# Delta rule of a hybrid layer: the preparations of two pairs of heads made together instead of one after the other

## The chip, the core and the metric

The kernel runs on one core of one Trainium2 chip. The core has a matmul engine (PE, with its weight loads shown apart as PEld), VectorE (DVE), ScalarE (ACT), GpSimd (POOL), and queues that issue DMA transfers (SPq, ACTq). All data are float32. The metric is the device time of one execution in microseconds (us), lower is better.

## The reference

The layer has two token mixers behind one normalisation and one input projection: a gated delta rule of 4 heads, and a dilated attention of 8 heads. Their outputs, each gated, go through one output projection and are added to the input. The sequence has 2048 tokens and 1024 channels. The change touches the delta rule alone. For each head it works on 32 chunks of 64 tokens:

```python
gc = jnp.cumsum(g.reshape(b, h, n, CHUNK), axis=-1)
diff = gc[..., :, None] - gc[..., None, :]
decay = jnp.exp(jnp.where(tril_incl, diff, -jnp.inf))
kb = kc * bc[..., None]
a_mat = jnp.where(tril_strict, jnp.einsum('bhnid,bhnjd->bhnij', kb, kc) * decay, 0.0)
l_mat = a_mat + jnp.eye(CHUNK, dtype=a_mat.dtype)
u = lax.linalg.triangular_solve(l_mat, vc * bc[..., None], ...)
w = lax.linalg.triangular_solve(l_mat, kb * jnp.exp(gc)[..., None], ...)
attn_intra = jnp.einsum('bhnid,bhnjd->bhnij', qc, kc) * decay
...
def step(state, inp):
    v_new = u_i - w_i @ state
    o_i = qd_i @ state + a_i @ v_new
    state = state * gl_i + kt_i.T @ v_new
```

Here `l_mat` is a 64x64 triangular matrix per chunk and head. The chunks of a head follow each other through `state`.

## The kernel before

The 4 heads are two pairs. The two heads of a pair lie side by side on the 128 partitions (64 each, `s_` counts them), and 4 chunks (`u`) are prepared at a time, so there are 8 groups of 4 chunks for each pair. The work has these stages.

1. **The input projection** (`conv_proj`, lines 460 to 481, and `gate_proj`): 128x128x512 products on PE, lines 206 to 208 (tile `pj`), then the short convolution on DVE and ACT.
2. **The products k k** (`stage1a`, lines 501 to 533), run while the projection goes on: for one pair and 4 chunks, k is loaded (`kT1`, one buffer), 8 products of 64 columns each go into one PSUM bank of tile `A` (line 514), and DVE makes the decayed matrix from it. It is called 16 times.
3. **The inverse** (`inverse`, lines 535 to 554): of each 64x64 triangular matrix the two 32x32 diagonal blocks are inverted, on DVE for the first half of the sequence and on POOL for the second, and stored to memory.
4. **The preparation** (`stage2`, lines 614 to 711), for one pair and 4 chunks at a time, 16 times. It loads k, q, v, the decays and the blocks of the inverse into `TTz` (line 643) and `D0t` (line 644). `TTz` exists twice, one for each call in turn, so in effect one for each pair. The missing 32x32 block of the inverse takes two products: 8 products of 32x32 (line 650), a copy by DVE (`Xs`, line 653), 8 more products (line 657), and a copy by ACT with a minus sign into `TTz` (line 660). Then come q k (line 665), the norms of q (line 668, in the bank of the 32x32 products), transposes of k and v (line 688), and the two products with the inverse (lines 701 and 707), the second of which reads `TTz` last. All of these use tile `A` of the pool `psD`, which has two PSUM banks. Its results `WQ`, `Ks`, `U` and `at_` have three buffers each.
5. **The chain** (`chain`, lines 720 to 747): for each chunk and pair, products with the state (line 727), new values (DVE, line 731), the state's update (PE line 733, DVE line 737), and the output (PE line 741, ACT and DVE). The update products of both pairs share one bank, `SU`.
6. **The attention**, whose projection (`proj_fill`, tile `pj`, issued through the helper at line 99) fills PE while the delta rule runs. At most 5 x 192 of its products may be issued before the last product of the chain (`HOLD`, lines 963 and 964). After that the attention's own steps begin, and then the output projection.

The order of the instructions on each engine is fixed when the kernel is compiled: a scheduler takes, among the instructions that it holds to be ready by its own estimate of times, the one of the highest priority (the lowest number in `tc.cur_priority`). Chain and outputs start from 1,000,000, the preparation from 1,200,000, the attention's projection from 2,400,000. From the attention on (`pin[0] = True`, line 839) the order within each engine is as written. `add_manual_dep(..., NOSYNC)` sets the order of two instructions of one engine and adds no wait.

The loop that starts the preparations (lines 783 to 793) runs over the groups: the chain's first chunk of both pairs, then the next group's preparation for pair 0 and for pair 1, then the other three chunks.

Of the kernel before, what the change touches and what calls it, by code (L numbers as in the profile page):

```python
# [8 lines left out]
F32 = mybir.dt.float32  # L9
# [7 lines left out]
P = 128  # L17
# [7 lines left out]
NOSYNC = mybir.DependencyInfo(mybir.DependencyClass.NoSync, mybir.DependencyReason.DATA)  # L25
CH = 64
# [54 lines left out]
def dap(t, off, dims):  # L81
    return bass.AP(tensor=t.tensor, offset=t.offset + off, ap=[list(d) for d in dims])


def hybrid(tc, xT, x, norm_w, w_in, conv_w, a_log, dt_bias, dn_norm_w, q_norm_w, k_norm_w,
# [37 lines left out]
    dma = nc.sync.dma_start  # L123
    adma = nc.scalar.dma_start

    dr, _ = pool("dr", space=DRAM)
    qkvT_d = [[dr.tile([P, 32, 2, CH], F32, name=f"cv{w}{p}") for p in range(2)] for w in range(3)]
# [91 lines left out]
    nc = engines  # L219
    dma = nc.sync.dma_start  # L220
    adma = nc.scalar.dma_start
# [4 lines left out]
    for _ in range(14):  # L226
# [5 lines left out]
                                                        bufs=3 if b + g < 2 else 1) for n in ("wh", "wl"))  # L232
# [94 lines left out]
    for kt in range(KT):  # L327
# [14 lines left out]
        for i in range(4):  # L342
            for j, (x_, w_) in enumerate(((xh, 0), (xh, 1), (xl, 0))):
                nc.tensor.matmul(pz[i][:, :260], x_[0][:, kt, i * P:(i + 1) * P], wz[0][kt][w_][:, kt % 4, :260],
                                 start=kt == 0 and j == 0, stop=kt == KT - 1 and j == 2)
# [4 lines left out]
    for g, (tb, b, i) in enumerate(groups):  # L350
# [12 lines left out]
        k = g if tb == 0 else (g - 4) % 8  # L363
# [21 lines left out]
    nc = tc.nc  # L385
    dma = nc.sync.dma_start
    adma = nc.scalar.dma_start
# [12 lines left out]
    at = ba[:, 4:8, :]  # L400
# [57 lines left out]
    mid, mid_g = pool("mid", side="right")  # L458
# [39 lines left out]

    psD, psD_g = pool("psD", space=PSUM)

    def stage1a(pair, c0):
        hf, cc = divmod(c0, 16)
        u0 = pair * 32 + c0
        kT = mid.tile([P, 4, 2, CH], F32, name="kT1", bufs=1)
        dma(kT, qkvT_d[1][pair][:, c0:c0 + 4])
        gcr = mid.tile([P, 4 * CH], F32, name="t0", bufs=2)
        for s_ in range(2):
            dma(gcr[s_ * CH:(s_ + 1) * CH, :],
                dap(rows_d, (2 * pair + s_) * S + c0 * CH, [[0, CH], [1, 256]]))
        kk = psD.tile([P, 4, CH], F32, name="A", bufs=2)  # L510
        for u in range(4):
            for s_ in range(2):
                ks = kT[:, u, s_]
                nc.tensor.matmul(kk[s_ * CH:(s_ + 1) * CH, u, :], ks, ks, start=True, stop=True)
        pr0 = tc.cur_priority
        tc.cur_priority = pr0 + PE1A
        a4 = mid.tile([P, 4 * CH], F32, name="t1", bufs=2).rearrange("p (u i) -> p u i", u=4)
        E = mid.tile([P, 4 * CH], F32, name="t2", bufs=3).rearrange("p (u i) -> p u i", u=4)
        for u in range(4):
            nc.vector.tensor_tensor_reduce(out=a4[:, u], in0=kk[:, u], in1=id64, scale=1.0, scalar=0.0,  # L520
                                           op0=ALU.mult, op1=ALU.add, accum_out=ssqk[:, u0 + u:u0 + u + 1])
            nc.vector.scalar_tensor_tensor(E[:, u], gcr[:, u * CH:(u + 1) * CH], gc_u[:, u0 + u:u0 + u + 1], mneg,
                                           op0=ALU.subtract, op1=ALU.add)
        nc.scalar.activation(E, E, AF.Exp)
        sA = sA_u[:, u0:u0 + 4]
        nc.vector.tensor_scalar(sA, ssqk[:, u0:u0 + 4], EPS, None, op0=ALU.add)
        nc.vector.reciprocal(sA, sA)
        nc.vector.tensor_tensor(sA, sA, beta_u[:, u0:u0 + 4], op=ALU.mult)
        nc.vector.tensor_tensor(E, E, sA[:, :, None].to_broadcast([P, 4, CH]), op=ALU.mult)
        nc.vector.tensor_tensor(a4, kk, E, op=ALU.mult)  # L530
        dma(A_d[hf][pair, cc:cc + 4].rearrange("u p i -> p u i"), a4)
        dma(Es_d[hf][pair, cc:cc + 4].rearrange("u p i -> p u i"), E)
        tc.cur_priority = pr0
# [23 lines left out]
    for hf in range(2):  # L557
        tc.cur_priority = PR1A[hf]
        for c in range(0, 16, 4):
            for p_ in range(2):  # L560
                stage1a(p_, hf * 16 + c)
        tc.cur_priority = PRINV[hf]
        inverse(hf)

    close(mid_g)
    mid, mid_g = pool("mid2", side="right")
# [14 lines left out]
    dn, dn_g = pool("dn")  # L581
# [29 lines left out]
    turn2 = [0]  # L611
    SU = psD.tile([P, 4, P], F32, name="SU", bufs=1)

    def stage2(pair, c0, dma2=dma):

        hf, cc = divmod(c0, 16)
        u0 = pair * 32 + c0
# [3 lines left out]
        kT = dn.tile([P, 4, 2, CH], F32, name="kT", bufs=2)  # L623
        qT = dn.tile([P, 4, 2, CH], F32, name="qT", bufs=2)
        vT = dn.tile([P, 4, 2, CH], F32, name="vT", bufs=1)
# [4 lines left out]
        for s_ in range(2):  # L630
            d0 = dma(Qr[:, :, s_], dap(rows_d, (12 + 2 * pair + s_) * S + c0 * CH, [[0, P], [CH, 4], [1, CH]]))
        WQ = dn.tile([P, 4, 2, P], F32, name="WQ", bufs=3)
# [3 lines left out]
        E = dn.tile([P, 4, CH], F32, name="E2", bufs=2)  # L636
        dma2(E, Es_d[hf][pair, cc:cc + 4].rearrange("u p i -> p u i"))
        TT = TTz[n2 % 2]
        D0 = dn.tile([P, 4, 32], F32, name="D0t", bufs=2)
        Xs = dn.tile([P, 4, 32], F32, name="Xs", bufs=1)  # L640
        for s_ in range(2):
            a = s_ * CH
            dma2(TT[a:a + CH, :, a:a + CH], A_d[hf][pair, cc:cc + 4, a:a + CH].rearrange("u p i -> p u i"))
            dma2(D0[a:a + 32], dap(D0_d[hf], (m0 + s_) * 1024, [[32, 32], [2048, 4], [1, 32]]))
        pa = psD.tile([P, 512], F32, name="A", bufs=2)
        px, pn = pa[:, :256].rearrange("p (a u i) -> p a u i", a=2, u=4), pa[:, 256:260]
        for u in range(4):
            for s_ in range(2):
                a, b = s_ * CH, s_ * CH + 32
                nc.tensor.matmul(px[b:b + 32, 0, u], TT[a:a + 32, u, b:b + 32], D0[a:a + 32, u], start=True, stop=True)  # L650
        for s_ in range(2):
            b = s_ * CH + 32
            nc.vector.tensor_copy(Xs[b:b + 32], px[b:b + 32, 0])
        for u in range(4):
            for s_ in range(2):
                a, b = s_ * CH, s_ * CH + 32
                nc.tensor.matmul(px[a:a + 32, 1, u], Xs[b:b + 32, u], TT[b:b + 32, u, b:b + 32], start=True, stop=True)
        for s_ in range(2):
            a = s_ * CH
            nc.scalar.mul(TT[a:a + 32, :, a + 32:a + 64], px[a:a + 32, 1], -1.0)  # L660
        q2 = dn.tile([P, 4, P], F32, name="tmp", bufs=2)
        nc.scalar.activation(q2, qT.rearrange("p u s i -> p u (s i)"), AF.Square)
        pq = psD.tile([P, 4, P], F32, name="A", bufs=2)
        for u in range(4):
            nc.tensor.matmul(pq[:, u], kT[:, u].rearrange("p s i -> p (s i)"), qT[:, u].rearrange("p s i -> p (s i)"),  # L665
                             start=True, stop=True)
        for u in range(4):
            nc.tensor.matmul(pn[:, u:u + 1], q2[:, u], one, start=True, stop=True)
        at_ = dn.tile([P, 4, P], F32, name="at_", bufs=3)
        nc.gpsimd.memset(at_[:CH, :, :CH], 0.0)  # L670
        nc.gpsimd.memset(at_[CH:, :, CH:], 0.0)
        for s_ in range(2):
            a, b = slice(s_ * CH, (s_ + 1) * CH), slice((1 - s_) * CH, (2 - s_) * CH)
# [6 lines left out]
        Ks = dn.tile([P, 4, 2, P], F32, name="Ks", bufs=3)  # L680
# [4 lines left out]
        for w, src in enumerate((kT, vT)):  # L685
# [3 lines left out]
            if w == 0:  # L689
                for u in range(4):  # L690
                    nc.scalar.mul(Kc[:, u], tp[:, u], negc_u[:, u0 + u:u0 + u + 1])
                for s_ in range(2):
                    a = slice(s_ * CH, (s_ + 1) * CH)
# [8 lines left out]
        for s_ in range(2):  # L702
            a = slice(s_ * CH, (s_ + 1) * CH)
# [4 lines left out]
        U = dn.tile([P, 4, P], F32, name="U", bufs=3)  # L708
        nc.scalar.copy(U, pu)
        o4 = dn.tile([P, 4, P], F32, name="o4", bufs=2)  # L710
        return dict(WQ=WQ, at=at_, Ks=Ks, U=U, o4=o4, D0=d0)

    Sst = []
    mark = {}
# [57 lines left out]
    def at_prio(k, f, *args):  # L772
        tc.cur_priority = prio[k]
        r = f(*args)
        prio[k] = tc.cur_priority
        return r

    G = {}
    last_D0 = []
    for p_ in range(2):  # L780
        G[p_] = at_prio("prep", stage2, p_, 0, adma)
    last_D0 = [G[1]["D0"]]
    for c0 in range(0, 32, 4):
        cur = dict(G)
        for u in range(4):
            for p_ in range(2):
                at_prio("chain", chain, p_, c0 + u, cur[p_])
            if u == 0:
                for p_ in range(2):
                    if c0 + 4 < 32:  # L790
                        G[p_] = at_prio("prep", stage2, p_, c0 + 4)
        for p_ in range(2):
            z = at_prio("out", dn_out, p_, c0, cur[p_])
        if c0 < 12:
            at_prio("out", bias_out, c0 // 4, z)
# [44 lines left out]
    nc = engines  # L840
    dma = nc.sync.dma_start
    adma = nc.scalar.dma_start
# [393 lines left out]
    G = [heads(hf, p) for hf in range(2) for p in range(4)]  # L1236
# [5 lines left out]
    at, at_g = pool("at")  # L1242
# [23 lines left out]
    for i, g in enumerate(G):  # L1266
        b = 12 * i
# [216 lines left out]
    g = G[7]  # L1484
# [11 lines left out]
    last, part = {}, {}  # L1496
# [56 lines left out]
```

## Time and profile before

| what | value |
|---|---|
| median of 3 runs | 1397.85 us (1396.52 to 1399.55) |
| the profiled execution's own time | 1397.04 us |
| its span, first to last instruction | 1395.2 us |
| DVE busy | 855.7 us (61%) |
| ACT busy | 677.6 us (49%) |
| POOL busy | 486.2 us (35%) |
| k k products on PE (line 514) | 162.2 to 322.9 us of the span |
| delta rule, preparations and chain | 456.5 to 778.5 us of the span |

The profile gives, for one execution, the busy time of each engine, who waited for whom, the chain of work that ended last, and a timeline of instructions. In the timeline an entry starts with its start time and its length in us; "x16" is sixteen records merged into one entry. A float32 product of this stage leaves two records. Products on PE overlap: each lasts longer than the distance to the next one's start, so what a product costs is read from start to start, and not from its length. The projection's products (lines 206 to 208 and `pj` at line 99) work on operands split in two parts and leave one record each.

### The profile page before, as it was taken

The page shows a single profiled execution, that of the slowest core. Times are in us where ns is not written, and L with a number is a line of the kernel's source. Part 1 is how long each engine was busy: PE and PEld are TensorE (multiplying, and loading weights), DVE is VectorE, ACT ScalarE, POOL GpSimd, SP SyncE. Part 2 cuts the span into 40 slices and gives each one's busy share as a digit, 9 for nine tenths or more (in the row PEclk, how much of TensorE's full clock was granted, in tenths as well). Part 3 has the DMA queues.
Part 4 walks back from the last instruction along what each step waited for, and adds up shares of the span by engine and source line. Part 5 has one row for each costly group of instructions (what it writes and reads, how often), then busy time and mean ns, then how long its engine had stood idle before and what let it go on. Part 6 is the DMA issues. An engine that isn't in the chain of part 4 may idle for free.

```text
span 1395.2 us, 28823 instructions
## 1 busy us (share of the span) xinstructions
PE 1362.5 (98%) x10262; PEld 1216.4 (87%) x10262; DVE 855.7 (61%) x2724; ACT 677.6 (49%) x1930; POOL 486.2 (35%) x572
## 2 busy tenths in 40 slices
PE   8999999999999999999999899999999999999998
PEld 7998787778888789999999889999998788888877
DVE  7535667799742358777787564635454746556464
ACT  5644425572321334444444476666556555555520
POOL 3000000000752113442343523575757385654500
PEclk9999999999999999999999999999999999999999
DMA  6654536756547736557553455273647685665764
GB/s 189 184 109 85 109 69 143 159 125 118 102 105 136 201 96 153 158 155 185 138 151 83 103 135 138 69 196 98 161 129 220 177 266 144 211 176 166 204 187 145
DMA packets 301323, 205.01 MB, mean 147 GB/s; under 512 B 149323, under 2 KB 271067, under 8 KB 300668
## 3 DMA queue, kind: packets, MB, share of 16 engines
q1 hardware_dynamic: 231372, 171.11, 49.6%
q10 hardware_dynamic: 69808, 32.06, 8.4%
q8 instruction: 81, 1.33, 0.4%
q14 instruction: 62, 0.51, 0.1%
HBM read 142.61 MB, written 60.50 MB: 146 GB/s over the span
## 4 chain that ended last, share of the span: by engine, by line
PE 80%; DVE 7%; DMA 4%; ACT 3%; POOL 2%; issue 2%; SPq 1%; ACTq 0%; DVEq 0%; POOLq 0%
PE pj L99 16%; PE po L99 10%; PE pj L207 7%; PE pj L208 7%; PE pj L206 7%; PE sc L99 7%; PE pz L99 6%; PE pv L99 4%; PE pt L99 4%; PE SU L733 2%; PE C L727 2%; ACT pr L99 1%; POOL Fb L99 1%; PE A L665 1%; PE pm L99 1%
## 5 line engine op out<-in xcount | busy, mean ns | idle before, releaser
L99 ACT ACTIVATE pr<-pr,ml 128x192 f32<-128x192 f32 (+2 forms) x384 | 156.8, 410 | 160.8 <-DVE ml L99 155.9
L99 PE MATMUL pj<-wh,xh 128*128 128x256 f32 (+1 forms) x776 | 227.1, 293 | 3.6 <-DVE t L99 2.3
L99 PE MATMUL pj<-wh,xl 128*128 128x256 f32 (+1 forms) x776 | 224.6, 289 | 0.0
L99 PE MATMUL pj<-wl,xh 128*128 128x256 f32 (+1 forms) x776 | 224.3, 289 | 0.0
L208 PE MATMUL pj<-xh,wl 128*128 128x512 f32 x512 | 203.5, 397 | 0.7 <-DVE wl L192 0.7
L206 PE MATMUL pj<-xh,wh 128*128 128x512 f32 x512 | 202.6, 396 | 0.0
L207 PE MATMUL pj<-xl,wh 128*128 128x512 f32 x512 | 202.6, 396 | 0.0
L99 PE MATMUL po<-xh,mh 128*128 128x512 f32 x424 | 148.5, 413 | 5.3 <-ACT mh L99 4.2
L99 PEld LDWEIGHTS pj<-wh,xh 128*128 128x128 f32 x776 | 146.4, 189 | 5.0 <-DVE t L99 2.7
L99 DVE CUSTOM_DVE_ANT_0 pr<-sc,bias 128x192 f32<-128x192 f32 (+2 forms) x384 | 100.1, 308 | 77.6 <-PE sc L99 76.7
L99 PEld LDWEIGHTS pj<-wh,xl 128*128 128x128 f32 x776 | 146.5, 189 | 0.5 <-issue 0.3
L99 PEld LDWEIGHTS pj<-wl,xh 128*128 128x128 f32 x776 | 146.6, 189 | 0.1
L478 DVE SCALAR_TENSOR_TENSOR cy<-cu,cw,cy 128x512 f32<-128x512 f32 x144 | 112.1, 778 | 19.8 <-ACT cy L476 17.8
L208 PEld LDWEIGHTS pj<-xh,wl 128*128 128x128 f32 x512 | 96.2, 188 | 23.4 <-DVE wl L192 1.1
L207 PEld LDWEIGHTS pj<-xl,wh 128*128 128x128 f32 x512 | 96.2, 188 | 22.1
L206 PEld LDWEIGHTS pj<-xh,wh 128*128 128x128 f32 x512 | 96.3, 188 | 21.7
L99 POOL COPY qz<-q 64x512 f32<-64x512 f32 x96 | 95.8, 998 | 54.0 <-PE sc L99 43.9
L99 DVE COPY pT<-pt 64x128 f32<-64x128 f32 (+2 forms) x220 | 69.4, 323 | 62.6 <-PE pt L99 59.1
L99 PEld LDWEIGHTS po<-xh,mh 128*128 128x128 f32 x424 | 78.0, 189 | 19.4 <-ACT mh L99 4.8
L99 POOL TENSOR_TENSOR Fb<-Fb,op 128x256 f32<-128x256 f32 x84 | 71.6, 866 | 60.1 <-DMA Fb<-F 59.5
L543 POOL MEMSET inv<- 128x1024 f32 x1 | 1.0, 955 | 260.0 <-ACT wh L191 260.0
L99 PE MATMUL po<-xl,mh 128*128 128x512 f32 x212 | 86.9, 410 | 0.0
(369 smaller groups left out, 3066.3 us busy)
## 6 DMA issues: line engine op xcount, KB each, us to landing
wraw<-in_w_in SPq DMA_DIRECT2D x44, 512.0 KB, 7.2
cv<-cy ACTq DMA_DIRECT2D x48, 256.0 KB, 2.6
Fb<-F SPq DMA_DIRECT2D x64, 192.0 KB, 5.6
xr<-in_xT SPq DMA_DIRECT2D x32, 256.0 KB, 4.0
kT<-cv SPq DMA_DIRECT2D x32, 256.0 KB, 3.5
qk<-qs ACTq DMA_DIRECT2D x64, 128.0 KB, 4.0
res<-in_x SPq DMA_DIRECT2D x13, 512.0 KB, 5.5
V<-v_d SPq DMA_DIRECT2D x20, 256.0 KB, 4.1
```

Of the source, the lines that this page charges most:

```text
L99: i = f(*args, **kw)
L206: nc.tensor.matmul(ps, wh[:, k, c * P:(c + 1) * P], xh[tb][:, kt, :], start=kt == 0, stop=False)
L207: nc.tensor.matmul(ps, wh[:, k, c * P:(c + 1) * P], xl[tb][:, kt, :], start=False, stop=False)
L208: nc.tensor.matmul(ps, wl[:, k, c * P:(c + 1) * P], xh[tb][:, kt, :], start=False, stop=kt == KT - 1)
L478: nc.vector.scalar_tensor_tensor(y, u[:, i:i + 512], cw[:, ct, i:i + 1], y, op0=ALU.mult, op1=ALU.add)
L543: eng.memset(Tt, 0.0)
L665: nc.tensor.matmul(pq[:, u], kT[:, u].rearrange("p s i -> p (s i)"), qT[:, u].rearrange("p s i -> p (s i)"), start=True, stop=True)
L727: nc.tensor.matmul(pc[:, s_], g["WQ"][:, u, s_], S0[:, s_], start=True, stop=True)
L733: nc.tensor.matmul(su[:, s_], g["Ks"][:, u, s_], VN, start=True, stop=True)
```

## The change

Three things are done for both pairs at once that were done for one pair at a time.

- The k k products of both pairs (32 records where there were 16) go into one PSUM bank of tile `A` in a new function `stage1k`; `stage1a` gets its half of the bank. `kT1` has two buffers instead of one.
- `stage2` is split into `stage2_load`, `stage2_blocks` and `stage2_rest`. The loads of both pairs come first, then the 32x32 products of both, then the rest of pair 0 and the rest of pair 1.
- In `stage2_blocks` the 16 first products (line 650 before), those of pair 1 ahead of those of pair 0, and the 16 second products (line 657 before) are each tied in order with `add_manual_dep(..., NOSYNC)`. One copy by DVE for each half of the partitions takes both pairs' blocks. Both pairs' norms of q lie in that same bank, which comes free when both have been read.

```diff
-    def stage1a(pair, c0):
+    def stage1k(c0):
+        kk = psD.tile([P, 2, 4, CH], F32, name="A", bufs=2)
+        for pair in range(2):
+            kT = mid.tile([P, 4, 2, CH], F32, name="kT1", bufs=2)
+            dma(kT, qkvT_d[1][pair][:, c0:c0 + 4])
+            for u in range(4):
+                for s_ in range(2):
+                    ks = kT[:, u, s_]
+                    nc.tensor.matmul(kk[s_ * CH:(s_ + 1) * CH, pair, u, :], ks, ks, start=True, stop=True)
+        return kk
+
+    def stage1a(pair, c0, kk):
-        kT = mid.tile([P, 4, 2, CH], F32, name="kT1", bufs=1)
-        dma(kT, qkvT_d[1][pair][:, c0:c0 + 4])
+        kk = kk[:, pair]
-        kk = psD.tile([P, 4, CH], F32, name="A", bufs=2)
-        for u in range(4):
-            for s_ in range(2):
-                ks = kT[:, u, s_]
-                nc.tensor.matmul(kk[s_ * CH:(s_ + 1) * CH, u, :], ks, ks, start=True, stop=True)
...
-    def stage2(pair, c0, dma2=dma):
+    def stage2(c0, dma2=dma):
+        g = [stage2_load(p_, c0, dma2) for p_ in range(2)]
+        stage2_blocks(g)
+        return [stage2_rest(p_, c0, g[p_]) for p_ in range(2)]
+
+    def stage2_load(pair, c0, dma2):
...
+    def stage2_blocks(g):
         pa = psD.tile([P, 512], F32, name="A", bufs=2)
-        px, pn = pa[:, :256].rearrange("p (a u i) -> p a u i", a=2, u=4), pa[:, 256:260]
+        px = pa[:, :256].rearrange("p (w u i) -> p w u i", w=2, u=4)
+        Xs = dn.tile([P, 2, 4, 32], F32, name="Xs", bufs=1)
+        last = []
+
+        def row(m):
+            if last:
+                tc.add_manual_dep(m.ins, last[-1].ins.name, NOSYNC, reason="in a row")
+            last.append(m)
+
+        for w in (1, 0):
+            TT, D0 = g[w]["TT"], g[w]["D0_"]
+            for u in range(4):
+                for s_ in range(2):
+                    a, b = s_ * CH, s_ * CH + 32
+                    row(nc.tensor.matmul(px[b:b + 32, w, u], TT[a:a + 32, u, b:b + 32], D0[a:a + 32, u], start=True,
+                                         stop=True))
         for s_ in range(2):
             b = s_ * CH + 32
-            nc.vector.tensor_copy(Xs[b:b + 32], px[b:b + 32, 0])
+            nc.vector.tensor_copy(Xs[b:b + 32], px[b:b + 32])
+        for w in range(2):
+            TT = g[w]["TT"]
+            g[w]["pn"] = pa[:, 256 + 4 * w:260 + 4 * w]
+            for u in range(4):
+                for s_ in range(2):
+                    a, b = s_ * CH, s_ * CH + 32
+                    row(nc.tensor.matmul(px[a:a + 32, w, u], Xs[b:b + 32, w, u], TT[b:b + 32, u, b:b + 32], start=True,
+                                         stop=True))
+        for w in range(2):
             for s_ in range(2):
-                a, b = s_ * CH, s_ * CH + 32
-                nc.tensor.matmul(px[a:a + 32, 1, u], Xs[b:b + 32, u], TT[b:b + 32, u, b:b + 32], start=True, stop=True)
...
+                a = s_ * CH
+                nc.scalar.mul(g[w]["TT"][a:a + 32, :, a + 32:a + 64], px[a:a + 32, w], -1.0)
+
+    def stage2_rest(pair, c0, g):
...
-    for p_ in range(2):
-        G[p_] = at_prio("prep", stage2, p_, 0, adma)
+    G[0], G[1] = at_prio("prep", stage2, 0, adma)
...
-                for p_ in range(2):
-                    if c0 + 4 < 32:
-                        G[p_] = at_prio("prep", stage2, p_, c0 + 4)
+                if c0 + 4 < 32:
+                    G[0], G[1] = at_prio("prep", stage2, c0 + 4)
```

More of the change, by code (lines that the diff above doesn't have):

```diff
@@ L559, in hybrid @@
         for c in range(0, 16, 4):
+            kk = stage1k(hf * 16 + c)
             for p_ in range(2):
-                stage1a(p_, hf * 16 + c)
+                stage1a(p_, hf * 16 + c, kk)
         tc.cur_priority = PRINV[hf]
@@ L644, in stage2 @@
             dma2(D0[a:a + 32], dap(D0_d[hf], (m0 + s_) * 1024, [[32, 32], [2048, 4], [1, 32]]))
+        return dict(kT=kT, qT=qT, vT=vT, WQ=WQ, E=E, TT=TT, D0_=D0, D0=d0)
+    def stage2_blocks(g):
         pa = psD.tile([P, 512], F32, name="A", bufs=2)
-        px, pn = pa[:, :256].rearrange("p (a u i) -> p a u i", a=2, u=4), pa[:, 256:260]
-        for u in range(4):
-            for s_ in range(2):
-                a, b = s_ * CH, s_ * CH + 32
-                nc.tensor.matmul(px[b:b + 32, 0, u], TT[a:a + 32, u, b:b + 32], D0[a:a + 32, u], start=True, stop=True)
+        px = pa[:, :256].rearrange("p (w u i) -> p w u i", w=2, u=4)
[12 more added lines that the diff above has]
+                                         stop=True))
@@ L651, in stage2 @@
         for s_ in range(2):
             b = s_ * CH + 32
-            nc.vector.tensor_copy(Xs[b:b + 32], px[b:b + 32, 0])
-        for u in range(4):
-            for s_ in range(2):
[L656 to L660, printed above, removed]
+            nc.vector.tensor_copy(Xs[b:b + 32], px[b:b + 32])
@@ L661, in stage2 @@
+    def stage2_rest(pair, c0, g):
+        hf, cc = divmod(c0, 16)
+        u0 = pair * 32 + c0
+        kT, qT, vT, WQ, E, TT = (g[k] for k in ("kT", "qT", "vT", "WQ", "E", "TT"))
+        pn = g["pn"]
         q2 = dn.tile([P, 4, P], F32, name="tmp", bufs=2)
@@ L710, in stage2 @@
         o4 = dn.tile([P, 4, P], F32, name="o4", bufs=2)
-        return dict(WQ=WQ, at=at_, Ks=Ks, U=U, o4=o4, D0=d0)
+        return dict(WQ=WQ, at=at_, Ks=Ks, U=U, o4=o4, D0=g["D0"])
     Sst = []
```

## The prediction

> **What bounds the kernel now.** I read the page first, for the engine that sets the pace.
>
> ```profile
> span 1395.2 us, 28823 instructions
> PE 1362.5 (98%) x10262; PEld 1216.4 (87%) x10262; DVE 855.7 (61%) x2724; ACT 677.6 (49%) x1930; POOL 486.2 (35%) x572
> ```
>
> PE is busy nearly all the time. Since products overlap, that says only that PE is never long without one. So I asked for the busy times of three stretches (columns: stretch, its length, then busy time and count of PE, PEld, DVE, ACT, POOL, the granted clock, DMA), and for the waits of PE from 150 to 800 us (time in total, times, longest).
>
> ```profile
> 150.00:330.00 180.00, 178.88 (x969) 141.20 (x968) 143.32 (x471) 91.97 (x114) 0.00 (x0) 1.00 0.59 125
> 520.00:766.00 246.00, 246.00 (x2411) 240.63 (x2407) 190.00 (x581) 111.91 (x364) 92.15 (x132) 1.00 0.58 145
> 766.30:778.30 12.00, 8.58 (x58) 6.81 (x56) 10.27 (x32) 3.60 (x14) 2.84 (x3) 1.00 0.49 56
> ```
> ```profile
> PE A L650 <- DMA D0t<-D: 1.8, 1, 1.8
> ```
>
> The first stretch holds the k k products, the second nearly all of the delta rule, the third its end. From 520 to 766 PE waits for nobody, at full clock, with DVE at 190 of 246 us. In these two stages the time is the sum of what PE's instructions cost from start to start: an instruction made cheaper there is time won, and a faster DVE, ACT or POOL is worth nothing. The third stretch is the exception: the attention's products are used up (the mark in the projection forbids more), and the last chunks of the chain run alone. PE issues 58 records there; at 0.11 us each (from the rows below) that is 6.4 of the 12.0 us, so 5.6 us are lost. The longest single wait of the delta rule is 1.8 us, at the first 32x32 product, for a load.
>
> **The edits, one by one.** No product is removed: the same records are regrouped. So what counts is what a group costs beside its records. First the k k products:
>
> ```profile
> 220.23 0.40 PE L207 MATMUL pj<-xl,wh 128*128 128x512 f32 x1
> 220.46 0.39 PE L208 MATMUL pj<-xh,wl 128*128 128x512 f32 x1
> 220.78 0.69 PE L514 MATMUL A<-kT 128*64 128x64 f32 x16
> 221.40 0.50 PE L206 MATMUL pj<-xh,wh 128*128 128x512 f32 x1
> 221.74 0.39 PE L207 MATMUL pj<-xl,wh 128*128 128x512 f32 x1
> ```
> ```profile
> 162.17 0.57 PE L514 MATMUL A<-kT 128*64 128x64 f32 x12
> 162.67 0.50 PE L208 MATMUL pj<-xh,wl 128*128 128x512 f32 x1
> ...
> 322.49 0.69 PE L514 MATMUL A<-kT 128*64 128x64 f32 x16
> ```
>
> Large products follow each other by 0.23 us (220.23 to 220.46). Into the row the step is 0.32, so 0.09 more; the row takes 0.62; the step after the first large product behind it is 0.34, 0.11 more. A row of 12 takes 0.50 (162.17 to 162.67), so four records cost 0.12, 0.03 each; sixteen make 0.48, and 0.14 of the 0.62 is not theirs. A row costs 0.09 + 0.14 + 0.11 = 0.34 us beside its records. The timeline has 17 such rows, the first at 162.17 and the last at 322.49. Joined they are 8, since both pairs' loads lie well ahead of the bank that they wait for: 9 x 0.34 = **3.1 us saved**. The second `kT1` buffer removes a wait that hardly shows. The bank is held longer, but DVE, which empties it, does the same work in the same order.
>
> Now the 32x32 products.
>
> ```profile
> L650 PE MATMUL A<-D0t,TTz 32*32 32x32 f32 x256 | 8.1, 194 | 1.8 <-DMA D0t<-D 1.8
> L657 PE MATMUL A<-TTz,Xs 32*32 32x32 f32 x256 | 7.9, 194 | 0.0
> ```
> ```profile
> 555.52 0.61 PE L727 MATMUL C<-S,WQ 128*128 128x128 f32 x4
> 555.97 0.61 PE L707 MATMUL A<-tmp,TTz 128*128 128x128 f32 x4
> 556.51 0.44 PE L650 MATMUL A<-D0t,TTz 32*32 32x32 f32 x16
> 556.88 0.38 PE L99 MATMUL pj<-wh,xh 128*128 128x256 f32 x1
> 557.10 0.28 PE L99 MATMUL pj<-wl,xh 128*128 128x256 f32 x1
> 557.22 0.28 PE L99 MATMUL pj<-wh,xl 128*128 128x256 f32 x1
> ```
> ```profile
> 456.54 0.21 PE L650 MATMUL A<-D0t,TTz 32*32 32x32 f32 x2 [1.78 <-DMA D0t<-D]
> ...
> 597.02 0.31 PE L657 MATMUL A<-TTz,Xs 32*32 32x32 f32 x6
> ...
> 598.12 0.37 PE L657 MATMUL A<-TTz,Xs 32*32 32x32 f32 x10
> ...
> 744.51 0.24 PE L657 MATMUL A<-TTz,Xs 32*32 32x32 f32 x2
> 744.68 0.94 PE L665 MATMUL A<-qT,kT 128*128 128x128 f32 x6
> ```
>
> There are 16 x 8 products of each kind, two records each. Four records of 128x128 take 0.45 (555.52 to 555.97), 0.11 each; before the row they take 0.54, so 0.09 for going in. The row takes 0.37. Behind it a step is 0.22 where 0.12 is usual: 0.10. A row of two takes 0.17 (744.51 to 744.68), so fourteen records more cost 0.20, 0.0143 each; sixteen make 0.23, and 0.14 of 0.37 is not theirs. One row costs 0.09 + 0.14 + 0.10 = 0.33 us beside its records, more than the records themselves. The Trainium skill, "TensorE: Matmul & The Clock Gate", section "Wait — 56ns, not 53.3ns?", has a floor that would halve this: starts never come closer than about 25 ns, however small the product. By it sixteen records would use up the whole 0.37, a row would cost only 0.19, and the saving below would be 3.6 us; the trace does not agree, with 14 ns per record between the two rows.
>
> The timeline has 41 rows of 32x32 products, the first at 456.54 and the last at 744.51: 32 would do, and 9 of them are cut in two or more, as the one at 597.02 is by products of the chain, which have the higher priority. After the change 16 would do. The tie between neighbours fixes their order but keeps nothing else out, and a row twice as long is cut more often; I take 22. That is 19 x 0.33 = **6.3 us saved** (bounds: 41 rows as now, 0; 16 rows, 8.3).
>
> The `Xs` copies by DVE become half as many and twice as wide, hidden behind PE, as DVE's 190 of 246 us allow.
>
> **What the joining adds.** First, the row now needs the blocks of both pairs. In the first group the second pair's loads are issued on ACT's queue behind the first pair's:
>
> ```profile
> 458.33 0.61 ACTq L644 DMA_DIRECT2D D0t<-D  x1
> ```
>
> By the shortest landing of this line, 1.6 us, that is not there before 459.9, where the row now starts at 456.54. Queued behind it stand all later products; some of the projection can be placed ahead. Between 0 and 4.5 us more waiting: I take **1.5 us lost**, nearest to the 1.78 already there.
>
> ```profile
> L644 ACTq DMA_DIRECT2D D0t<-D x4: 310/613/2042, 447.3 to 458.3; - x4
> ...
> DMA to landing us min/median/max: 1.6/2.8/9.1
> ```
>
> Second, in every later group. `TTz` of pair 1 is read last by line 707, the last product of a preparation. Before, that tile was reloaded while the other pair was prepared, well ahead of its use. Now the joint row of the next group needs it at once. What that takes:
>
> ```profile
> 592.00 0.61 PE L707 MATMUL A<-tmp,TTz 128*128 128x128 f32 x4
> ...
> 592.89 0.44 PE L650 MATMUL A<-D0t,TTz 32*32 32x32 f32 x16
> ```
> ```profile
> 592.64 1.25 SPq L643 DMA_DIRECT2D TTz<-A  x2
> ```
> ```profile
> L643 SPq DMA_DIRECT2D TTz<-A x28: 573/588/1572, 476.9 to 722.8; - x28
> ...
> DMA to landing us min/median/max: 2.3/4.5/9.2
> ```
>
> The next row could so far start 0.45 us behind the last product; now two loads of 0.6 us issue and a landing of 2.3 to 9.2 us lie between. The compile-time order fills that time with the attention's products, but for a landing that it estimates; if the transfer is later, PE stands still with everything behind the row. At nothing if the estimate is generous or the two banks of `A` are busy anyway with the next q k products; at 4.5 - 2.3 = 2.2 us if it counts on the shortest landing and gets the median. Seven groups: 0 to 15 us. I take a third of a microsecond each, **2.5 us lost**, nearer to zero because no other wait of PE stands between 520 and 766.
>
> Third, the end. Of the 5.6 us lost there, some come back if the delta rule's latency falls: four dependent steps fewer in a group (row, copy, row, ACT copy are made once for both). I take **2.5 us saved**, bounds 0 and 5.6; a longer delta rule is the rivals' matter.
>
> **Sum.** -3.1 - 6.3 + 1.5 + 2.5 - 2.5 = -7.9 us. The profiled execution took 1397.04 us (span 1395.2 and 1.8 around it), so 1389.1; the median of the runs lies 0.8 above that execution, which gives **1389.9 us**.
>
> **Rivals.**
>
> *The reload decides (slower).* Each of the seven later rows waits the 2.2 us, nothing is won at the end: -9.4 + 1.5 + 15.4 = +7.5, 1405 us. For it: the first row did wait 1.78 us for just such a load, and landings reach 9.2 us. Against it: an order laid out by the same estimates lets PE wait for no load and no engine between 520 and 766. It decides from 1.1 us a group on, (9.4 - 1.5) / 7. Chance 0.18.
>
> *The rows do not stay whole.* If the chain cuts the longer rows as often per record as now, some 36 remain: 5 x 0.33 + 3.1 = 4.8 saved, less 4.0 of the two waits: 1397 us, no change. For it: 9 cuts now, and a tie that excludes nothing. Against it: most rows of sixteen are whole. Chance 0.16.
>
> *The delta rule gets clearly shorter.* Pair 1's preparation hangs now on the third buffer of `at_`:
>
> ```profile
> L674 DVE TENSOR_TENSOR at__5609<-A,E x2: 416/422/428, 600.2 to 600.6; 64x256 f32<-64x256 f32 x2
> ```
> ```profile
> 611.68 0.59 ACT L709 COPY U<-A 128x512 f32<-128x512 f32 x1 [0.54 <-PE A L707]
> ```
>
> From 600.2 to 612.3 the remaining steps of that pair take 12.1 us. With the blocks and norms of both pairs done early, several of them leave this path, the chain ends before the attention's products run out, and the whole 5.6 us come back, without stalls: -9.4 - 5.6 + 0.5 for the start = -14.5, 1383 us. Chance 0.12.
>
> **How the numbers follow.** The forecast has 0.54. Two thousandths, 2.8 us, is about what a measurement of this kernel can tell from no change. Faster by more: 0.50 of the forecast, 0.07 of the cut rows, 0.12 of the short delta rule: 0.69. Within: 0.04, 0.09 and 0.02 of the reload: 0.15. Slower: 0.16 of the reload. The range runs from 1382, just below the short delta rule, to 1399.5, which leaves out most of the reload's case and nothing else.
>
> **What would show it.** Right: PE waits for nobody from 520 us to the end of the chain but at the joint rows; about 8 rows of 32 k k records and some 22 rows of 32x32 records; a row of 32 takes about 0.60 us from start to start. The reload would show as waits of the first product on `TTz<-A` seven times. Cut rows show as 32x32 rows of less than 32 records between products of lines 727 to 741. A shorter delta rule shows as the attention's products running on past the last product of the chain. I am wrong if the time outside 150 to 790 us moves by more than 2 us, since nothing there is changed.

## The result, and the profile after

| | before | after |
|---|---|---|
| median | 1398.7 us (1396.52 to 1402.04, 4 runs) | 1440.26 us (1433.72 to 1445.3, 4 runs) |
| ratio, 95% interval | | 1.0292 [1.0245, 1.0339] |
| profiled execution | 1397.04 us, span 1395.2 | 1440.5 us, span 1438.7 |
| mean granted clock | 0.997 | 0.984 |

The change makes the kernel 41.6 us slower. The forecast was 1389.9 us, 8 us faster than before; its range ended at 1399.5. The sign was wrong, and the loss lies far beyond every case that the prediction named; the slowest of them was 1405 us.

The page of after, the first lines:

```profile
span 1438.7 us, 28759 instructions
PE 1377.7 (96%) x10262; PEld 1231.4 (86%) x10262; DVE 850.6 (59%) x2708; ACT 668.8 (46%) x1922; POOL 486.9 (34%) x572
```

PE has the same number of records as before, and is busy for 15.2 us more in a span that is 43.5 us longer. The next view, busy times by stretch, says where. The stretch runs from 440 us to the last product of the chain, which ends at 819.2 us where it was 778.3. Columns as in the prediction: stretch, length, busy time and count of PE, PEld, DVE, ACT, POOL, granted clock, DMA. First before, then after.

```profile
440.00:778.30 338.30, 333.10 (x3011) 314.04 (x3009) 236.15 (x705) 140.83 (x442) 112.10 (x163) 1.00 0.59 144
```
```profile
440.00:819.20 379.20, 345.30 (x2989) 324.09 (x2988) 229.83 (x685) 141.15 (x440) 111.47 (x157) 0.95 0.52 127
```

This stretch became 40.9 us longer and holds nearly the whole loss; behind it the kernel takes 619.5 us where it took 616.9. PE's idle time went from 338.30 - 333.10 = 5.2 us to 33.9: 28.7 us more. Its busy time went up by 12.2 us though the stretch holds 22 records fewer: the clock column has 0.95 where it had 1.00. The waits of PE from 440 to 820 us name the instruction:

```profile
PE A L676 <- DMA TTz<-A: 14.9, 4, 5.0
PE A L676 <- DMA D0t<-D: 4.9, 2, 4.0
PE A L676 <- issue: 4.4, 2, 4.2
PE A L739 <- ACT tmp L736: 3.0, 2, 1.7
```

Line 676 is the first joint row (line 650 before). In all it waits 24.2 us, where the prediction's view had one wait of 1.8. Most of it is for `TTz`, the tile whose reload the prediction had taken at 0.36 us a group. The sign of the reload was to be seven such waits. There are four, and a fifth of 4.2 us (at 555.81) that the view can put down to nothing (`issue`); the rows that begin at 511.17 and 692.47 had no such wait. One of the four, in the timeline of PE and in that of the SP queue:

```profile
638.94 1.06 PE L745 MATMUL A<-tmp,TTz 128*128 128x128 f32 x8
...
643.82 0.28 PE L99 MATMUL pj<-wh,xh 128*128 128x256 f32 x1
649.05 0.28 PE L676 MATMUL A<-D0t,TTz 32*32 32x32 f32 x2 [4.96 <-DMA TTz<-A]
649.27 1.65 PE L703 MATMUL A<-qT,kT 128*128 128x128 f32 x6
```
```profile
641.21 1.26 SPq L792 DMA_DIRECT2D zs<-zs_d  x2
642.57 0.57 SPq L99 DMA_DIRECT2D wraw<-in_w_in  x1
643.24 1.24 SPq L655 DMA_DIRECT2D TTz<-A  x2
```

Pair 1's last product (line 745) has read its tile at 640.0. Three other transfers stand ahead of the reload on the queue, which issues at 643.24 and again some 0.6 later, and the row starts at 649.05. From the last product to the row that is 9 us. Until 644.10 the attention's products fill it; the row's place in the order comes then, and PE stands for 5 us. In the waits of the SP queue from 440 to 830 us the reload stood seven times for line 745, 32.7 us in all.

Such a wait can cost more than its length. The granted clock behind the wait that ends at 737.9 us, in stretches of about 2 us of PE alone:

```profile
735.20:737.90 2.70, 0.21 (x2) 0.93 0.75 220
737.90:740.00 2.10, 2.07 (x35) 0.50 0.08 17
740.00:742.00 2.00, 2.00 (x11) 0.50 0.38 81
742.00:744.00 2.00, 2.00 (x12) 0.50 0.53 58
744.00:746.00 2.00, 2.00 (x17) 0.91 0.99 79
```
```profile
511.17 0.69 PE L676 MATMUL A<-D0t,TTz 32*32 32x32 f32 x32
...
737.93 1.06 PE L676 MATMUL A<-D0t,TTz 32*32 32x32 f32 x30 [2.52 <-DMA TTz<-A]
```

For some 6 us behind the wait PE runs at half speed. The timeline shows the same in the rows: 32 records without a wait are 0.69 us long, 30 records behind one 1.06. How long it lasts differs: the wait that ends at 602.66 was as long (2.51 us), but there the clock stayed at 1.00 until about 604.4 and was at 0.50 only until 607.8. These stretches of half speed are the 0.95 of the whole.

Last, the end of the stage:

```profile
766.00:819.20 53.20, 38.51 (x320) 33.40 (x318) 40.54 (x138) 20.37 (x80) 9.68 (x13) 0.94 0.35 78
```

The attention's products are used up at about 765 us, as before. But then the chain still has 53 us to go where it had 12. The groups come every 44 us, and the last 53 us have nothing left to fill PE's gaps. Until 765 us the lateness of the groups showed only in the waits and the clock; here it shows in full.

### The profile page after: what moved, and what is told of

Read it like the earlier page. It is cut to its first block, busy times and chain, and to the rows that moved or that the text cites. A ratio compares the mean times of both kernels' runs of the same rounds, so it can differ in the third digit from the quotient of the medians.

```text
span 1438.7 us, 28759 instructions
## 1 busy us (share of the span) xinstructions
PE 1377.7 (96%) x10262; PEld 1231.4 (86%) x10262; DVE 850.6 (59%) x2708; ACT 668.8 (46%) x1922; POOL 486.9 (34%) x572
## 4 chain that ended last, share of the span: by engine, by line
PE 77%; DMA 7%; DVE 6%; ACT 3%; POOL 3%; issue 2%; SPq 1%; ACTq 0%; DVEq 0%; POOLq 0%
PE pj L99 14%; PE po L99 9%; PE pj L206 8%; PE pj L208 8%; PE pj L207 8%; PE sc L99 6%; PE pz L99 5%; PE pv L99 4%; PE pt L99 4%; PE SU L771 2%; PE C L765 2%; DMA TTz<-A 2%; POOL Fb L99 1%; PE A L703 1%; DVE xl L99 1%
```

## The experiments

All kernels compute the whole layer. Every ratio is to before, timed on the same one of three chips; before had medians of 1398.6 to 1399.0 us there. A difference in us between two kernels of different chips is good to some tenths of a us at best.

**k k products alone.** The part in `stage1k` and `stage1a` is taken over into the kernel before, and nothing else.

```diff
-    def stage1a(pair, c0):
+    def stage1k(c0):
...
-                stage1a(p_, hf * 16 + c)
+                stage1a(p_, hf * 16 + c, kk)
```

> The kernel before with only the k k products of both pairs joined in one bank. The working of the prediction gives 9 rows x 0.34 us = 3.1 us less: 1395.6 us, ratio 0.998. The rival: the delta rule's start is set by something other than PE's work (the span to the first 32x32 product was the same in both traces, 454.4 and 454.6 us), then the saved time only lets other products move forward and the total falls by the same 3 us later or not at all: ratio 1.000.

Measured: 1395.32 us (1393.42 to 1397.71), ratio 0.9979 [0.9970, 0.9989]: 3.4 us saved by the medians. A joined row in its timeline:

```profile
220.48 1.15 PE L510 MATMUL A<-kT 128*64 128x64 f32 x32
221.56 0.50 PE L208 MATMUL pj<-xh,wl 128*128 128x512 f32 x1
```

From start to start 32 records take 1.08 us; two rows of 16 took 2 x 0.62, and went in and out twice. The rival was that something other than PE's work sets the start of the delta rule. The first 32x32 product starts at 453.7 us here, at 456.5 before (and at 455.9 in after; the two times in the expectation are not those of that product), so the saved time does move the start. This part does what it was said to do, and the loss is all in the delta rule.

**Loads of both first, rows pair by pair.** From after: `stage2_load` for both pairs stays ahead, but each pair has its own bank, rows, copies and rest, with no ties.

```diff
-        stage2_blocks(g)
-        return [stage2_rest(p_, c0, g[p_]) for p_ in range(2)]
+        done = []
+        for p_ in range(2):
+            stage2_blocks(g[p_])
+            done.append(stage2_rest(p_, c0, g[p_]))
+        return done
```

> The changed kernel with one part undone: the loads of both pairs still come first and the k k products are joined, but the 32x32 products, their copy and the rest are done for pair 0 and then for pair 1, each with its own bank. If the joined rows are the cause (through reload, bank or anything else), 1394 to 1398 us. If the order of the loads is a cause, above 1402 us.

Measured: 1394.81 us (1392.37 to 1398.87), ratio 0.9970 [0.9957, 0.9983]. Not to be told from the k k part alone. Splitting `stage2` and loading early costs nothing that shows; joining the rows, with the shared bank that goes with it, does.

**A third `TTz` tile.** With three tiles in turn, pair 1 of the next group takes the tile that pair 0 of this one gave back half a group earlier, and no reload waits for pair 1's last product. In the first attempt the room came from the second buffer of the gate `zs`.

```diff
-    TTz = [dn.tile([P, 4, P], F32, name=f"TTz{i}") for i in range(2)]
+    TTz = [dn.tile([P, 4, P], F32, name=f"TTz{i}") for i in range(3)]
...
-    TT = TTz[n2 % 2]
+    TT = TTz[n2 % 3]
...
-        zs = dn.tile([P, 4, P], F32, name="zs", bufs=2)
+        zs = dn.tile([P, 4, P], F32, name="zs", bufs=1)
```

> The changed kernel with a third tile for the blocks of the inverse, so that the reload of a pair no longer waits for the last product of the same group (paid for in memory by one buffer of the gate tile instead of two). Theory 1, the reload: the waits of the joint rows (24 us in the page of the changed kernel) and the slower clock behind them are gone, and the delta rule is as short as before: 1392 to 1400 us. Theory 2, the bank: the bank with the blocks and both pairs' norms of q is held from the first row to the norms of pair 1 (649 to 677 us in one group), pair 0 has one bank for all its products, and the delta rule stays long: the waits go but 1415 to 1428 us remain.

Measured: 1413.54 us, ratio 1.0106 [1.0087, 1.0124], between the two expectations and in neither. 27 us of the loss are gone, and no wait of PE for `TTz` is left. But the single gate buffer makes a wait of its own, on DVE (waits in total, times, longest):

```profile
DVE zs L800 <- DMA zs<-zs_d: 13.5, 5, 3.7
```

So this run changed two things, and shows only that the reload costs a good part of the loss.

**The third tile from a buffer that lies idle.** The pool `mid` has a third 2 KB buffer, `big`, that nothing uses until the attention's first loads of its input (`big<-in_xT`, from 707.0 us in after); `zs` keeps both of its own.

```diff
+    TTz.append(mid.tile([P, 512], F32, name="big", bufs=3).rearrange("p (u i) -> p u i", u=4))
...
-    TT = TTz[n2 % 2]
+    TT = TTz[n2 % 3]
```

> The changed kernel with the third tile of the inverse again, but taken from a buffer of the attention's pool that lies idle during the delta rule, so that the gate tile keeps its two buffers (the first try made DVE wait 13.5 to 23.7 us for gate loads, in front of the chain's work). Theory 1, the reload alone: 1392 to 1400 us, the delta rule ends by 780 us of the span. Theory 2, the bank held for pair 1's norms as well: 1402 to 1410 us, groups of 32x32 rows 38 to 40 us apart instead of 37.

Measured: 1404.56 us, ratio 1.0039 [1.0024, 1.0054]. One more tile takes back 35.7 of the 41.6 us. The time is that of theory 2, the distance of the rows that of theory 1. The only wait of the joint row left is in the first group, and the groups follow each other as in before (waits of PE, then the timeline, second and eighth group):

```profile
PE A L677 <- DMA D0t<-D: 4.0, 2, 2.6
```
```profile
510.95 0.44 PE L677 MATMUL A<-D0t,TTz 32*32 32x32 f32 x16
...
732.96 0.44 PE L677 MATMUL A<-D0t,TTz 32*32 32x32 f32 x16
```

Six groups in 222.0 us are 37.0 each; before, 556.51 to 592.89 in the prediction's rows, 36.4, and 36.8 in the mean of six (519.63 to 740.27). A rival would be that the waiting reload holds up the transfers behind it in the SP queue. But the queue still stands before the reload for 27.3 us here (32.7 in after), and in after PE's only waits for loads are those of line 676, for `TTz` and in the first group for `D0t`. So the gain is the reload's own.

**Norms of both pairs early.** The second suspect is the bank that holds the blocks and norms of both pairs. In after, one hold of it on ACT and DVE (it begins with the row at 649.05):

```profile
672.35 0.63 ACT L700 ACTIVATE tmp<-qT 128x512 f32<-128x512 f32 x1 [0.40 <-PE A L739]
```
```profile
665.82 0.14 DVE L713 COPY ssqq<-A 128x4 f32<-128x4 f32 x1
...
677.04 0.16 DVE L713 COPY ssqq<-A 128x4 f32<-128x4 f32 x1 [0.20 <-PE A L706]
```

Pair 0's norms are read at 665.8. Pair 1's squares of q need one of the two `tmp` tiles, which come free only with pair 0's w product (line 739), so its norms are read at 677.0. The bank is held for 28 us; meanwhile all other products of the preparation share one bank. The edit makes the norms of both pairs right behind the rows.

```diff
+        for w in range(2):
+            q2 = dn.tile([P, 4, P], F32, name="tmp", bufs=2)
+            nc.scalar.activation(q2, g[w]["qT"].rearrange("p u s i -> p u (s i)"), AF.Square)
+            for u in range(4):
+                nc.tensor.matmul(g[w]["pn"][:, u:u + 1], q2[:, u], one, start=True, stop=True)
+        for w in range(2):
+            nc.vector.tensor_copy(ssqq[:, w * 32 + c0:w * 32 + c0 + 4], g[w]["pn"])
...
-        nc.vector.tensor_copy(ssqq[:, u0:u0 + 4], pn)
```

> The changed kernel with the norms of q of both pairs made and read right behind the 32x32 products, so that their bank comes free early; the two tiles of the inverse stay. Theory 1, the reload: the rows still wait, 1430 to 1440 us. Theory 2, the bank: the groups follow each other faster by some 5 to 8 us, 7 groups, though the rows still wait: 1400 to 1415 us.

Measured: 1417.51 us, ratio 1.0144 [1.0125, 1.0164]: 22.7 us taken back, with the two `TTz` tiles as they are. That is 2.5 us above the range of theory 2, and well below that of theory 1.

```profile
PE A L676 <- DMA D0t<-D: 4.5, 2, 3.6
PE A L676 <- DMA TTz<-A: 4.3, 5, 2.6
...
PE A L676 <- issue: 2.8, 2, 1.9
```
```profile
508.30 0.24 PE L676 MATMUL A<-D0t,TTz 32*32 32x32 f32 x2
...
750.17 0.22 PE L676 MATMUL A<-D0t,TTz 32*32 32x32 f32 x2 [1.85 <-issue]
```

The reload still stands in the way, but shorter: six groups in 241.9 us, 40.3 each, against 44.4 in after (five groups from 511.17 to 733.10). Theory 2 had said 5 to 8 us a group; it is 4.1. The edit also puts the squares on ACT and the norms' products on PE earlier. What of the 22.7 us is the bank alone was not separated.

**Both, with the single gate buffer.** The edits of the first attempt and of the norms together.

```diff
-    TT = TTz[n2 % 2]
+    TT = TTz[n2 % 3]
...
+        for w in range(2):
+            nc.vector.tensor_copy(ssqq[:, w * 32 + c0:w * 32 + c0 + 4], g[w]["pn"])
...
+        zs = dn.tile([P, 4, P], F32, name="zs", bufs=1)
```

> Both edits together: third tile of the inverse and norms made early. If reload and bank both matter, this is the first version in which the saved row costs (9.4 us in the prediction's working) can show: 1385 to 1393 us. If only the reload matters, the same as with the third tile alone; if only the bank, the same as with the early norms alone.

Measured: 1418.8 us, ratio 1.0145 [1.0130, 1.0160]. A miss: I expected the two gains to add up, and the time is that of the early norms alone, above that of the third tile alone. The waits of DVE and of PE point to the gate buffer:

```profile
DVE zs L801 <- DMA zs<-zs_d: 23.7, 6, 8.4
```
```profile
PE SU L772 <- DVE VN L770: 9.9, 7, 5.1
```

DVE stands in its queue before the gate's product, which waits for its load, up to 8.4 us; the chain's new values are queued behind it, and PE waits for those. The next run, with both gate buffers, bears this out.

**Both, with the idle buffer.** The norms early, the third tile from `big`, two gate buffers.

```diff
+    TTz.append(mid.tile([P, 512], F32, name="big", bufs=3).rearrange("p (u i) -> p u i", u=4))
...
-    TT = TTz[n2 % 2]
+    TT = TTz[n2 % 3]
...
+        for w in range(2):
+            nc.vector.tensor_copy(ssqq[:, w * 32 + c0:w * 32 + c0 + 4], g[w]["pn"])
```

> Third tile from the idle buffer and the norms of both pairs made early. If reload and bank are the whole cause, the 9.4 us of the rows show at last: 1386 to 1394 us. If it stays above 1400 us, joining the rows costs by something else: the first pair's products wait for the second pair's data and steps, and the chain with them.

Measured: 1402.36 us (1400.34 to 1407.63), ratio 1.0023 [1.0010, 1.0037]. With both suspects gone 37.9 of the 41.6 us are back, but the time is above 1400 us: the gain that was expected did not show. Waits of PE, then rows from the timeline:

```profile
PE SU L773 <- DVE S L777: 2.9, 3, 1.4
...
PE SU L773 <- DVE VN L771: 1.3, 2, 1.0
PE A L677 <- DMA D0t<-D: 0.9, 1, 0.9
```
```profile
504.44 0.44 PE L677 MATMUL A<-D0t,TTz 32*32 32x32 f32 x16
504.72 0.42 PE L677 MATMUL A<-D0t,big 32*32 32x32 f32 x16
505.07 1.16 PE L708 MATMUL A<-qT,kT 128*128 128x128 f32 x8
...
720.19 0.44 PE L677 MATMUL A<-D0t,TTz 32*32 32x32 f32 x16
```

The groups come every 36.0 us, the clock is 0.99 from 520 to 766 us, and a whole row of 32 takes 0.63 us. The timeline has 26 rows of 32x32 products where before had 41. From its first row to the last product of the chain the delta rule takes 318.0 us, 3.8 less than before. Yet the kernel is 7 us slower than with the k k part alone.

Where these 7 us are, the two profiles show in part. The joined row starts 6.2 us later than the first row of the k k kernel (459.85 and 453.66), the delta rule is some 4 us shorter, and its end is 2.2 us later (777.8 and 775.6). Another 4.3 us lie behind that end, where nothing was changed. There the views of the same stretch differ in the granted clock, first the k k kernel, then this one:

```profile
925.60:1075.60 150.00, 143.01 (x1295) 136.78 (x1294) 74.21 (x324) 92.98 (x331) 94.14 (x97) 1.00 0.56 150
```
```profile
927.80:1077.80 150.00, 142.63 (x1258) 136.75 (x1257) 71.08 (x312) 89.80 (x319) 88.65 (x94) 0.96 0.54 145
```

The mean granted clock of the ten runs of this kernel is 0.989 to 0.994 (median 0.991), that of the twelve of the k k kernel 0.994 to 0.999 (median 0.9955). An estimate from these: 0.0045 of 1400 us is 6 us. So most of what is left goes with the clock; what lowers it in this kernel stays open.

**Control: the third tile in the k k kernel.** Could the tile itself do good or harm?

```diff
+    TTz.append(mid.tile([P, 512], F32, name="big", bufs=3).rearrange("p (u i) -> p u i", u=4))
...
-    TT = TTz[n2 % 2]
+    TT = TTz[n2 % 3]
```

> Control: the kernel before with the joined k k products and the third tile of the inverse, rows of 32x32 products per pair as before. Every theory says that the third tile does nothing where no row waits for a reload: 1394 to 1397 us, as with the joined k k products alone.

Measured: 1399.03 us, ratio 0.9995 [0.9979, 1.0010], above the expectation. Where the rows are apart a third tile brings nothing; it may cost a little, and I have no cause for that. One thing it does: the third of the attention's first loads into `big` now waits for the tile and is issued at 739.2 us, at 721.0 in the k k kernel; its first use comes only at 795.5, well behind. The tile's 35.7 us in after are a wait that the joining made.

**The first group apart.** What is left of the loss could be the first joint row, which waits for both pairs. Here only the first group goes pair by pair, the other seven as in the kernel with both edits.

```diff
+        if c0 == 0:
+            done = []
+            for p_ in range(2):
+                stage2_blocks1(g[p_], c0, p_)
+                done.append(stage2_rest(p_, c0, g[p_]))
+            return done
         stage2_blocks(g, c0)
```

> The joint kernel with a third TTz tile and the norms of both pairs right behind the joint rows, but the first group of the delta rule (tokens 0 to 3) done pair by pair, each with a bank of its own, as in rows_apart. Theory: what is left of the loss in tt3b_norms is the first joint row, which waits for the loads of both pairs; the delta rule then starts at about 453.5 us instead of 459.9, its length stays at about 318 us or gets 1 longer for the first rows, so the time falls by 5 to 6 us, to 1396 to 1398 (ratio to before about 0.998). Rival: the late start was not on the path, since the loads of the later groups set the end: the start moves to 453.5 and the delta rule gets longer by as much, the time stays within 2 us of 1402.4.

Measured: 1396.82 us (1392.49 to 1400.36), ratio 0.9984 [0.9972, 0.9997], 5.5 us less than the kernel with all groups joined. The start is best read against the last load's issue on ACT's queue, because the stages ahead of it end some us earlier or later from profile to profile. First the joined group, then the first group apart:

```profile
457.74 0.61 ACTq L657 DMA_DIRECT2D D0t<-D  x1
```
```profile
459.85 0.22 PE L677 MATMUL A<-D0t,TTz 32*32 32x32 f32 x2 [0.92 <-DMA D0t<-D]
```
```profile
458.83 0.61 ACTq L663 DMA_DIRECT2D D0t<-D  x1
```
```profile
457.05 0.22 PE L717 MATMUL A<-D0t,TTz 32*32 32x32 f32 x2 [2.01 <-DMA D0t<-D]
```

The joint row starts 2.1 us behind that issue, the single one 1.8 us ahead of it: 3.9 us. The start at 453.5 that I expected did not show, since in this profile the loads themselves were issued later. Its delta rule takes 320.4 us, 2.4 more than the joined one, so the two profiles end the delta rule at about the same time (777.4 and 777.8 us), as the rival said. The time, however, fell as the theory said. The gain stands in the runs, ten of the joined kernel and twelve of this one on another chip, and not in this pair of profiles; on this one's chip the kernel of the next experiment, which has all groups joined, stood at 1.0027. The median granted clock rose too, from 0.991 to 0.9945, so how much of the 5.5 us is the start stays open.

**Without the ties.** The kernel with both edits, the NOSYNC ties of the rows left out.

```diff
-            if last:
-                tc.add_manual_dep(m.ins, last[-1].ins.name, NOSYNC, reason="in a row")
```

> tt3b_norms without the ties that hold the 32 products of a row behind one another. Theory: the rows stay nearly whole or fall into pieces that the scheduler fills with other work; each further stretch of 32x32 products costs about 0.33 us, so with up to 41 stretches instead of 26 the delta rule gets up to 5 us longer, 1402 to 1407. Rival: the ties hold back the scheduler, work that could have gone between is late because of them; without them the delta rule is shorter in spite of more stretches, 1398 to 1401.

Measured: 1402.44 us, ratio 1.0027 [1.0014, 1.0040], the same as with them, and the rows are cut just as often (26 rows). The ties neither help nor hurt that can be measured. The time lies in the range of the theory, but the further rows that were to bring it there did not come, so this run could not tell the two expectations apart.

## Why the prediction was wrong

**What failed: the second point of what the joining adds.** It named the reload of pair 1's `TTz`, and saw that two issues of 0.6 us and a landing of 2.3 to 9.2 us now have to fit where the next row had followed the last product by 0.45 us. Then it took a third of a microsecond a group, "because no other wait of PE stands between 520 and 766". That was no evidence: the order of before never had to place a reload there. The third tile shows that the reload costs about 36 us, five a group, where 2.5 us were taken for all seven. The upper bound of 15 us and the rival at 1405 us were too small as well, for three reasons:

1. *A wait was priced once; it closes a loop.* In after each group waits for the one before: row, rest of pair 0, rest of pair 1, its last product, queue, reload, next row. All of it adds up to the period of 44.4 us. In before each pair had half a group of slack for its tile (the reload issued at 592.64 in the prediction's rows was needed at 613.65, the next row of that pair), and the period of 36 to 37 us was PE's own work. What lengthens a part of the loop now counts in every group. The two runs with the norms early fit this: that edit gains 22.7 us where the loop is closed, and 2.2 (1404.56 to 1402.36) where the third tile has opened it. The prediction did not price the bank of the delta rule at all.
2. *A wait of PE can take the clock with it.* Half speed for 3.4 to 6.8 us behind waits of 2.5 to 5 us: with it the busy time grew by 12.2 us in all, for which the sum had no term. By the Trainium skill, "TensorE: Matmul & The Clock Gate", section "HAM oscillation — how this bites in real kernels", a PE left idle by a wait for a load for over about 3.4 us is throttled to half and starts cold on its next work. The trace agrees on the half, not on the length: waits of 2.5 us were already enough. Nor is it sure: the attention has a wait of 2.45 us at about 1070 us, with which the clock stayed at 1.00 in the k k kernel, was 0.50 for 3.4 us in before, and 0.50 for 6.8 us in the kernel with both edits.
3. *The filling ran out.* The attention's products hid the lateness until 765 us and then no more. The third point counted 2.5 us saved at the end, and left a longer delta rule to the rivals; the end holds 53.20 - 38.51 = 14.7 of the 33.9 us of idle time.

**The first group.** Predicted 1.5 us lost, bounds 0 to 4.5. The rows above show the joint row 3.9 us later against the last load's issue, nearer to the upper bound: the loads of pair 1 are issued last, and the row starts behind them. The kernel with the first group apart is 5.5 us faster; how much of the 3.9 us is lost time stays open, as said there.

**The k k products.** Right: 3.1 us predicted, 3.4 measured (1.5 to 4.2 by the ratio's interval). There are 9 rows where 8 were counted; at the price of 0.34 us that makes 2.7, within the interval too.

**The 32x32 rows.** Their price was right: a row of 32 takes 0.63 us, predicted 0.60. The count was not: 36 in after where 22 were taken. That is the rival "the rows do not stay whole", and its number, though in part by luck: with both edits 26 remain, so ten of the cuts went with those edits, and the rival had named the chain alone. 15 fewer at 0.33 are 5.0 us, and the delta rule of that kernel is 3.8 shorter than before. So the gain is there but small, and in the profile the later first row takes nearly all of it back: the chain ends at 777.8 us, before at 778.3. With rows joined (first group apart) the kernel is at 0.9984, with rows apart at 0.9970 and 0.9979: the intervals overlap, as they do with the control that has the third tile and rows apart (0.9995). So the joining by itself has bought nothing that can be measured.

**The time outside.** Behind the chain's last product it moved by 2.6 us, just over the 2 us that I had allowed. The other kernels of this study scatter there from 616 to 623 us, with the clock stretches told above among the reasons, so I make nothing of it.

## What to carry to other kernels

Joining two alternating steps doubles what must be ready at once: ask of every buffer that the two used in turn when it was given back, and when it is now needed again. If the answer is "by the last step of the round" and "at the first of the next", the round has become a loop through the transfer; price it as a whole round, with the clock that PE can lose behind each wait, and with what is left to fill PE at the end, and give the join another buffer before trying it. A saving of a third of a microsecond a row is worth having only where it costs no wait at all.

## What the runs showed of the hardware

PE's clock fell to 0.50 near the end of a wait of 2.5 us and stayed there for some 6 us more, although PE was busy all that time (737.9 to about 744.4 us). Behind another wait as long it fell 1.7 us after PE had begun again, for 3.4 us (604.4 to 607.8). One and the same wait of 2.45 us in the attention left the clock alone in one kernel's profile and halved it for 3.4 or 6.8 us in others. A piece of 64 KB of the reload took from 2.1 to 9.0 us to land in after, and from 2.3 to 9.2 before: a wait on it cannot be planned closely.
